# Order of the weight requests, PSUM banks and store queue around the early up-projection products of a hybrid encoder layer

## The chip, the core and the metric

The kernel runs on one core of one Trainium2 chip, as one launch. The metric is the device time of an execution in microseconds (us), the median of several runs. All engine times below are from one profiled execution of the kernel.

The engines are named as the profile names them: PE is TensorE (matmuls and transposes), PEld its weight load, DVE is VectorE, ACT is ScalarE, POOL is GpSimd, SP is SyncE, which here only issues DMAs. A name with a q (SPq, ACTq, POOLq) is the engine's queue issuing a DMA.

## What is computed

One encoder layer on 1024 tokens of width 1024, in float32. A token mixer (a gated delta rule beside a latent attention, both out of one input projection) ends in an output projection; after it comes a dense squared-ReLU MLP. The part that matters here:

```python
mixed = jnp.concatenate([o_gdn, o_mla], axis=-1) @ w_out
x = x + rms_norm(mixed, mix_post_norm)
h = rms_norm(x, ffn_pre_norm)
f = jnp.square(jax.nn.relu(h @ w_up)) @ w_down      # w_up: 1024 x 4096
x = x + rms_norm(f, ffn_post_norm)
```

## The kernel before, in words

Each float32 matmul is done as three passes on split operands (`mm3`, lines 206 to 209): an operand is kept as a high part (hi, cast on ACT) and a low part (lo, the rest, subtracted on DVE), and hi x hi, hi x lo and lo x hi are added up in PSUM. So every weight block is loaded into a raw tile, then split (`split_of`, lines 1323 to 1327: line 1325 on ACT, line 1326 on DVE).

**Out-projection and norms** (`out_proj`, line 1232). The 1024 tokens are eight blocks t of 128. For each block the projection adds two halves of 512 columns, each in one PSUM bank with the tag "out" (blocks 0 and 1 have theirs done earlier). `out_add` (line 1170) then adds a half to `part[t]` on DVE (line 1172) and squares it on ACT back into the bank (line 1173), which ends the use of the bank. The post norm, the residual and the pre norm follow on DVE (lines 1243 to 1251); line 1251 leaves the input of the MLP in `part[t]` and ends the use of the tile `xt`.

**Transposes** (`ffn_in`, line 1280, and `put`, line 1264). The up-projection is done with a Strassen-Winograd scheme of seven products on halves of the tokens and of the model width. Its moving operands are B11 and B21 (from blocks 0 to 3), and T1, T2, T3, T4 and B22 (from differences of blocks 4 to 7 with blocks 0 to 3, DVE lines 1291 to 1304; line 1294 writes a tile t2). `put` transposes 128 x 512 with four PE transposes (line 1268) into one of two "tr" banks and splits it (line 1273 on ACT, line 1274 on DVE). For t from 4 to 7 `ffn_in` is a generator that yields after each of its five puts.

**Pairs and early products.** The 4096 columns of w_up are 16 pairs p of 256 columns, each with two rows of weight tiles (512 KB each), `w_up[2p]` and `w_up[2p+1]`. Two of the seven products need only B11 and B21. For the eight even pairs they are computed ahead, by `filler` (line 1346): it requests `w_up[2p]`, splits it, runs twelve matmuls on B11 into a "ps" bank, copies the bank back into the first half of the raw tile (line 1355) and stores that half in DRAM (line 1356), runs twelve more on B21 onto the same bank, applies ReLU and square into the second half of the raw tile (lines 1363 and 1364) and stores it too (line 1365). The raw tile is free when both stores have landed. `fillers` (line 1368) chains the eight generators, each with four yields, and requests and splits the next one's row before it starts one. A regular pair is `up_pair` (line 1412); it needs `load_up(p)` (line 1387, both rows) and `prepare(p)` (line 1390), which forms on DVE a tile of sums (lines 1398 and 1399) and two differences (lines 1402 and 1405) and splits them. An even pair fetches its early products from DRAM (lines 1417 and 1418) and runs the remaining five products of twelve matmuls.

**What sets the order.** The order of each engine's queue is made when the kernel is built, from the order of the text as priority and from what is ready, so that products of later generators can stand ahead of earlier ones. All weight requests go through `load_chained` (line 182), which keeps those on SP's queue in the order of the text. Three buffer groups matter:
- "raw" (line 956): three tiles of 512 KB;
- "g" (line 1221): six tiles of 512 KB, for the two gain rows `gb` and `gf`, the eight `xt`, the t2 of blocks 4 to 7, four tiles of T3 that stay to the end of the up-projection, `sums`, and every fourth raw tile: `raw_of` (line 1317) takes a "g" tile where its running number leaves 3 when divided by 4;
- the weight pairs of `pair_tiles` (line 1312), five in turn: three of "whi"/"wlo", then "first", then "wv".

PSUM has eight banks. `psum_pool("psC", ...)` (line 1213) shares them out for this stretch: two "out", two "tr", four "ps".

**The order around the change** (lines 1462 to 1483). Blocks 0 to 7 go through `out_proj`, with the puts of blocks 0 to 3 between them and four steps of the early products at blocks 6 and 7. Then come `load_up(0)` and `prepare(0)`; then the five puts of each of blocks 4 to 7 with one step of the early products behind each put, and behind block 5 two steps of `prepare(0)`; then the remaining steps of the early products, the rest of `prepare(0)`, and the regular pairs. By the running number of `raw_of` the requests are: 1 and 2 for the first two early products, 3 ("g") and 4 for pair 0, 5 and 6 for the next two early products, 7 ("g") to 10 for the other four, 11 ("g") and 12 for pair 1.

Of the kernel before, what the change touches and what calls it, by code (L numbers as in the profile page):

```python
# [104 lines left out]
def build(tc, a, out):  # L105
    nc = tc.nc
# [15 lines left out]
    def psum_pool(name, **bufs):  # L122
        ps_stack.close()
        pp[:] = [ps_stack.enter_context(tc.tile_pool(name=name, bufs=1, space=PSUM, reuse_waits="tile")), bufs]
        for tag in bufs:
            psum2("order") if tag == "ps2" else psum("order", tag)
# [3 lines left out]
    def psum(name, tag="ps"):  # L130
        return pp[0].tile([P, HALF], F32, name=name, tag=tag, bufs=pp[1][tag])

    def psum2(name):
        return pp[0].tile([P, 2, HALF], F32, name=name, tag="ps2", bufs=pp[1]["ps2"])
# [71 lines left out]
    def mm3(ps, lhs, rhs, start, stop, **kw):  # L206
        mm(ps, lhs[0], rhs[0], start=start, stop=False, **kw)  # L207
        mm(ps, lhs[0], rhs[1], start=False, stop=False, **kw)  # L208
        mm(ps, lhs[1], rhs[0], start=False, stop=stop, **kw)  # L209
# [5 lines left out]
    def scratch(name, *shape):  # L215
        return dp.tile(list(shape), F32, name=name)
# [17 lines left out]
    d_p1 = [scratch(f"d_p1{p}", P, HALF) for p in range(NFILL)]  # L234
# [741 lines left out]
    def filler():  # L976
        yield "v1"
        yield from keys_values()

    def latent_side():  # L980
# [11 lines left out]
        + [substitute()]  # L992
        + [levels(h) for h in range(GH)]
        + [scan_loads(), scan(), filler(), latent_side(), projections()]
    )
    LB.close()
# [213 lines left out]
            out_pairs(early[t][:, n], t, n, (NPAIR - 1,))  # L1210
            out_add(early[t][:, n], t, n, ss1[t])
    L.close()
    psum_pool("psC", out=2, tr=2, ps=4)


    L = ExitStack()
# [3 lines left out]
    def gtile(name, dt=F32):  # L1220
        return gp.tile([P, D], dt, name=name, tag="g", bufs=6)
# [38 lines left out]
    def moving(block, k):  # L1260
        n = 4 // len(block)
        return cut(block[k // n], slice(None), k % n)
# [13 lines left out]
    first_half, second_half = slice(0, HALF), slice(HALF, D)  # L1276
# [3 lines left out]
    def ffn_in(t):  # L1280

        h = part[t]
        if t < 4:
            put(B11, h[:, first_half], t)
            put(B21, h[:, second_half], t)
            return
        if t == 4:
            later.update(T1=big("T1", bp, "b"), B22=big("B22", bp, "b"), T2=halves_of("T2", mtile))
        o, c = part[t - 4], t - 4
        t2 = gtile("t2")[:, :HALF]  # L1290
        nc.vector.tensor_sub(o[:, first_half], h[:, first_half], o[:, first_half])
        put(later["T1"], o[:, first_half], c)
        yield
        nc.vector.tensor_sub(t2, h[:, second_half], o[:, first_half])
        put(later["T2"], t2, c)
        yield
        nc.vector.tensor_sub(o[:, second_half], o[:, second_half], t2)
        if t == 4:
            later.update(T4=halves_of("T4", mtile), T3=halves_of("T3", gtile))
        put(later["T4"], o[:, second_half], c)  # L1300
        yield
        put(later["B22"], h[:, second_half], c)
        yield
        nc.vector.tensor_sub(h[:, first_half], h[:, second_half], h[:, first_half])
        put(later["T3"], h[:, first_half], c)
        part[t] = part[t - 4] = None
        yield
# [9 lines left out]
    def raw_of(src):  # L1317
        raws[0] += 1
        r = gtile("raw") if raws[0] % 4 == 3 else raw_tile()
        load_chained(r, src)  # L1320
        return r

    def split_of(raw, n=D, eng=None):
        hi, lo = pair_tiles()
        nc.scalar.copy(hi[:, :n], raw)  # L1325
        (eng or nc.vector).tensor_tensor(lo[:, :n], raw, hi[:, :n].bitcast(F32), op=ALU.subtract)
        return hi, lo

    def k_slice(w, half, k):
        return cut(w, slice(None), slice(half * HALF + k * P, half * HALF + (k + 1) * P))  # L1330
# [12 lines left out]
    def early_pair(p):  # L1343
        return p % 2 == 0

    def filler(p):
        x = raw_of(a["w_up"][2 * p])
        w = split_of(x)
        yield
        ps = psum("ps_up")  # L1350
        for k in range(4):
            mm3(ps, k_slice(w, 0, k), moving(B11, k), k == 0, k == 3)
            if k == 1:
                yield
        nc.scalar.copy(x[:, first_half], ps)
        nc.gpsimd.dma_start(d_p1[p // 2], x[:, first_half])
        yield
        for k in range(4):
            mm3(ps, k_slice(w, 1, k), moving(B21, k), False, k == 3, skip_group_check=True)
            if k == 1:  # L1360
                yield
        square_of = x[:, second_half]
        nc.scalar.activation(square_of, ps, AF.Relu)
        nc.scalar.activation(square_of, square_of, AF.Square)
        nc.gpsimd.dma_start(act_block(p, 0), square_of)
        yield

    def fillers():
        gens = [filler(p) for p in range(NPR) if early_pair(p)]
        run(gens[0])  # L1370
        for n, g in enumerate(gens):
            run(gens[n + 1] if n + 1 < len(gens) else None)
            for _ in g:
                yield

    def act_block(p, j):
        return d_act[p // 2][j, :, (p % 2) * HALF : (p % 2 + 1) * HALF]
# [9 lines left out]
    def load_up(p):  # L1387
        loaded[p] = raw_of(a["w_up"][2 * p]), raw_of(a["w_up"][2 * p + 1])

    def prepare(p):  # L1390

        r1, r2 = loaded.pop(p)
        w = wts[p] = {}
        if not early_pair(p):
            w["A1"] = split_of(r1)
        yield
        s = gtile("sums")
        nc.vector.tensor_add(s[:, first_half], r2[:, first_half], r2[:, second_half])
        nc.vector.tensor_sub(s[:, second_half], s[:, first_half], r1[:, first_half])
        w["S12"] = split_of(s)  # L1400
        yield
        nc.vector.tensor_sub(r2[:, first_half], r1[:, first_half], r2[:, first_half])
        w["S3A"] = split_of(r2)
        yield
        nc.vector.tensor_sub(r1[:, second_half], r1[:, second_half], s[:, second_half])
        w["S4"] = split_of(r1[:, second_half], HALF)

    def run(g):
        if g is not None:
            next(g, None)  # L1410
# [51 lines left out]
    fill = fillers()  # L1462
    for t in range(NT):
# [4 lines left out]
        if t >= 6:  # L1468
            run(fill)
            run(fill)  # L1470
    load_up(0)
    ahead = prepare(0)
    for t in range(4, NT):
        for _ in ffn_in(t):
            run(fill)
        if t == 5:
            run(ahead)
            run(ahead)
    for _ in fill:
        pass  # L1480
    for _ in ahead:
        pass
    psum_pool("psD", ps=8)
# [54 lines left out]
    for p in range(NPR):  # L1538
        if p + 1 < NPR:
            ahead = prepare(p + 1)  # L1540
        else:
            ahead = None
# [160 lines left out]
```

## Time and profile before

| | us |
|---|---|
| median of three runs (1301.52 to 1306.1) | 1303.38 |
| profiled execution | 1300.08 |
| its span | 1298.4 |
| PE busy | 1229.7 (95% of the span) |
| DVE busy | 905.7 (70%) |
| ACT busy | 652.3 (50%) |
| POOL busy | 172.7 (13%) |
| mean granted PE clock | 0.979 of full speed |

In the stretch from 540 to 760 us the DMA view lists 20 requests of w_up rows by SP (512 KB each), eight stores of line 1356 by POOL (256 KB, 2.6 us from issue to landing in the median) and eight of line 1365 by POOL (256 KB, 2.9 us).

In a row of the timeline stand the start in us, the duration in us, the engine, the line, the operation, the tile written and the tiles read (buffer numbers left out), the shapes, and the count; in square brackets the idle time of the engine before it and what ended it. Lines 207, 208 and 209 are the three passes of `mm3`, so products are told apart by their tiles: a "ps_up" matmul that reads B11 or B21 belongs to an early product as long as the early products run, and one that reads T1 opens a regular even pair. In the chain of waits each row is a piece of the chain that ended last: its start, its length, and the work that it is. Matmuls overlap, so a matmul's step is read from the starts.

### The profile page before, as it was taken

Reading aid. Unit: us, or ns where it says so; the run is one execution under the profiler, and the core shown is the slowest. Engines: PE = TensorE matmul, PEld = TensorE weight load, DVE = VectorE, ACT = ScalarE, POOL = GpSimd, SP = SyncE. Lnnn points to the kernel's source line nnn. Section 1 sums busy time; section 2 is a strip of 40 time slices with the busy share of each in tenths; the row PEclk is TensorE's granted clock in tenths of the full one; section 3 lists DMA queues with packets and bytes.
Section 4 is the critical chain, followed back from the end, with each engine's and each line's share of the span. In section 5 each row is a group of like instructions: output and inputs, shape, how many; then the busy total and the mean of one; then the engine's idle time right before and its main releaser. Section 6 shows DMA issues by size and latency. Waiting matters only on the chain.

```text
span 1298.4 us, 17709 instructions
## 1 busy us (share of the span) xinstructions
PE 1229.7 (95%) x6224; PEld 1038.4 (80%) x6224; DVE 905.7 (70%) x1779; ACT 652.3 (50%) x1189; POOL 172.7 (13%) x168
## 2 busy tenths in 40 slices
PE   7999999999899899998777999999999999999995
PEld 6978888899778788877665888888887888888884
DVE  7678879546655876778955677677765686775844
ACT  6566743426655776754544354454445433344431
POOL 1011011220055443420001000000000000011021
PEclk9999999999999999999988999999999999999998
DMA  5114545645243511305523355555539984556802
GB/s 229 53 63 138 183 130 204 191 114 163 88 121 119 144 30 29 93 14 194 203 105 104 124 186 186 187 186 187 187 138 374 383 314 140 191 170 218 329 28 97
DMA packets 110193, 205.71 MB, mean 158 GB/s; under 512 B 33557, under 2 KB 51989, under 8 KB 110106
## 3 DMA queue, kind: packets, MB, share of 16 engines
q1 hardware_dynamic: 94848, 176.09, 40.4%
q10 hardware_dynamic: 13978, 24.31, 5.1%
q0 software_dynamic: 1280, 4.20, 0.8%
q8 instruction: 49, 0.80, 0.2%
q14 instruction: 38, 0.31, 0.1%
HBM read 143.07 MB, written 61.49 MB: 158 GB/s over the span
## 4 chain that ended last, share of the span: by engine, by line
PE 61%; DVE 4%; DMA 3%; issue 2%; ACT 2%; POOL 0%; SPq 0%; DVEq 0%; ACTq 0%; POOLq 0%
PE ps_dn L209 8%; PE ps_dn L208 8%; PE ps_up L207 7%; PE ps_dn L207 7%; PE ps_up L209 7%; PE ps_up L208 7%; PE ps_out L207 2%; PE ps_out L209 2%; PE ps_out L208 2%; PE ps_PT L1061 2%; PE ps_o L1080 1%; PE ps_sc L207 1%; DMA raw<-in_w_up_dram 1%; PE ps_o L1079 1%; PE ps_sc L208 1%
## 5 line engine op out<-in xcount | busy, mean ns | idle before, releaser
L1574 POOL TENSOR_TENSOR rows<-rows,gpost 128x512 f32<-128x512 f32 x16 | 23.9, 1512 | 553.3 <-ACT junk L1571 553.3
L209 PE MATMUL ps_proj<-hThi,wlo 128*128 128x512 f32 x192 | 75.1, 395 | 1.2 <-DVE wlo L199 1.2
L208 PE MATMUL ps_proj<-hTlo,whi 128*128 128x512 f32 x192 | 76.0, 396 | 0.0
L207 PE MATMUL ps_proj<-hThi,whi 128*128 128x512 f32 x192 | 76.0, 396 | 0.0
L1065 DVE TENSOR_TENSOR PTlo<-ps_PT,PThi 128x512 fp32r<-128x512 f32 (+2 forms) x96 | 52.0, 550 | 20.0 <-ACT PThi L1064 19.3
L1064 ACT CAST PThi<-ps_PT 128x512 fp32r<-128x512 f32 (+2 forms) x96 | 45.4, 481 | 29.9 <-PE ps_PT L1061 28.4
L1506 DVE TENSOR_TENSOR dlo<-draw,dhi 128x1024 fp32r<-128x1024 f32 x35 | 44.7, 1302 | 22.3 <-ACT dhi L1505 22.3
L208 PE MATMUL ps_dn<-dlo,dhi 128*128 128x512 f32 x144 | 56.0, 389 | 0.0
L209 PE MATMUL ps_dn<-dhi,dlo 128*128 128x512 f32 x144 | 56.0, 389 | 0.0
L207 PE MATMUL ps_dn<-dhi 128*128 128x512 f32 x144 | 55.5, 389 | 0.0
L1035 ACT ACTIVATE Pt<-ps_sc,nm 128x896 f32<-128x896 f32 (+3 forms) x64 | 48.0, 750 | 11.8 <-DVE nm L1033 7.6
L1325 ACT CAST whi<-raw 128x1024 fp32r<-128x1024 f32 (+1 forms) x28 | 24.9, 898 | 55.5 <-PE ps_up L208 54.0
L1505 ACT CAST dhi<-draw 128x1024 fp32r<-128x1024 f32 x35 | 36.1, 1048 | 33.1 <-issue 13.8
L1061 PE MATMUL ps_PT<-ident,Pt 128*128 128x128 f32 x288 | 46.4, 275 | 3.1 <-DVE PTlo L1065 1.8
L1033 DVE TENSOR_REDUCE nm<-ps_sc 128x1 f32<-128x896 f32 (+3 forms) x64 | 47.8, 750 | 1.2
L1040 POOL TENSOR_TENSOR Pt<-Pt,rs 128x128 f32<-128x128 f32 (+4 forms) x40 | 35.4, 884 | 88.5 <-DVE rs L1038 64.4
L199 DVE TENSOR_TENSOR wlo<-raw,whi 128x1024 fp32r<-128x1024 f32 (+1 forms) x27 | 33.9, 1259 | 17.8 <-ACT whi L198 15.2
L209 PEld LDWEIGHTS ps_proj<-hThi,wlo 128*128 128x128 f32 x192 | 36.1, 188 | 9.1 <-DVE wlo L199 1.7
L1079 PE MATMUL ps_o<-PThi,V 128*128 128x256 f32 (+1 forms) x160 | 40.5, 276 | 3.0 <-DVE o L1086 1.2
L208 PEld LDWEIGHTS ps_proj<-hTlo,whi 128*128 128x128 f32 x192 | 36.1, 188 | 7.4 <-issue 0.5
L207 PEld LDWEIGHTS ps_proj<-hThi,whi 128*128 128x128 f32 x192 | 36.1, 188 | 7.4 <-issue 0.5
L1061 PEld LDWEIGHTS ps_PT<-ident,Pt 128*128 128x128 f32 x288 | 34.0, 140 | 8.4 <-issue 2.4
(591 smaller groups left out, 3999.2 us busy)
## 6 DMA issues: line engine op xcount, KB each, us to landing
draw<-in_w_down_dram SPq DMA_DIRECT2D x47, 512.0 KB
draw<-d_act SPq DMA_DIRECT2D x41, 512.0 KB
raw<-in_w_up_dram SPq DMA_DIRECT2D x40, 512.0 KB
raw<-in_w_down_dram SPq DMA_DIRECT2D x17, 512.0 KB
raw<-in_w_qkvg_dram SPq DMA_DIRECT2D x16, 512.0 KB
d_act<-c SPq DMA_DIRECT2D x16, 512.0 KB
d_act<-s SPq DMA_DIRECT2D x16, 512.0 KB
raw<-d_act SPq DMA_DIRECT2D x15, 512.0 KB
```

The source lines that it names most:

```text
L207: mm(ps, lhs[0], rhs[0], start=start, stop=False, **kw)
L208: mm(ps, lhs[0], rhs[1], start=False, stop=False, **kw)
L209: mm(ps, lhs[1], rhs[0], start=False, stop=stop, **kw)
L1033: nc.vector.tensor_reduce(nm, ps[:, :npc, :w], axis=AX.XY, op=ALU.max, negate=True)
L1035: nc.scalar.activation(Pt[:, :n].rearrange("p (i w) -> p i w", i=npc), ps[:, :npc, :w], AF.Exp, bias=nm, scale=1.0, accum_out=sm)
L1040: nc.gpsimd.tensor_tensor(Pt[:, :n], Pt[:, :n], rs.to_broadcast([P, n]), op=ALU.mult)
L1061: transpose(ps[:, j * P : (j + 1) * P], Pt[:, b * P : (b + 1) * P], ident)
L1064: nc.scalar.copy(hi[:, :n, cs], ps3)
L1065: nc.vector.tensor_sub(lo[:, :n, cs], ps3, hi[:, :n, cs].bitcast(F32))
L1079: mm(ps[:, cs], V[h][:, b], hi[:, cs], start=(b == 0), stop=False)
L1505: nc.scalar.copy(hi, raw)
L1506: nc.vector.tensor_tensor(lo, raw, hi.bitcast(F32), op=ALU.subtract)
```

## The change

Three things are changed.
- The psC pool gives four banks to "out" and two to "ps"; "tr" keeps two.
- The two stores of each early product are issued by ACT instead of POOL.
- `load_up(0)` and `prepare(0)` move from ahead of the puts of block 4 to behind those of block 7 and one more step of the early products. Two steps of `prepare(0)` then go behind the next two steps of the early products, and the rest behind the last.

By the running number of `raw_of` the requests become: 1 and 2 for the first two early products, 3 ("g") to 6 for the next four, 7 ("g") and 8 for the last two, 9 and 10 for pair 0, 11 ("g") and 12 for pair 1.

```diff
@@ -1210,7 +1210,7 @@
     L.close()
-    psum_pool("psC", out=2, tr=2, ps=4)
+    psum_pool("psC", out=4, tr=2, ps=2)
@@ -1353,7 +1353,7 @@
         nc.scalar.copy(x[:, first_half], ps)
-        nc.gpsimd.dma_start(d_p1[p // 2], x[:, first_half])
+        nc.scalar.dma_start(d_p1[p // 2], x[:, first_half])
         yield
@@ -1362,7 +1362,7 @@
         nc.scalar.activation(square_of, ps, AF.Relu)
         nc.scalar.activation(square_of, square_of, AF.Square)
-        nc.gpsimd.dma_start(act_block(p, 0), square_of)
+        nc.scalar.dma_start(act_block(p, 0), square_of)
         yield
@@ -1468,16 +1468,15 @@
-    load_up(0)
-    ahead = prepare(0)
     for t in range(4, NT):
         for _ in ffn_in(t):
             run(fill)
-        if t == 5:
+    run(fill)
+    load_up(0)
+    ahead = prepare(0)
+    for n, _ in enumerate(fill):
+        if n < 2:
             run(ahead)
-            run(ahead)
-    for _ in fill:
-        pass
     for _ in ahead:
         pass
     psum_pool("psD", ps=8)
```

## Prediction

> **What bounds the kernel now.** The page shows TensorE (PE) busy in nearly every slice of the span, so time can be won only where PE waits. I therefore divided the stretch around the change into windows of 20 us. The columns are the window, then busy us and instructions of PE, PEld, DVE, ACT and POOL, then the granted PE clock, the DMA share and GB/s.
>
> ```profile
> 620.00:640.00 20.00, 19.35 (x90) 15.46 (x88) 19.71 (x48) 11.96 (x28) 1.81 (x3) 1.00 0.51 176
> 640.00:660.00 20.00, 13.71 (x52) 10.28 (x52) 16.22 (x33) 8.40 (x18) 1.62 (x3) 0.74 0.44 156
> 660.00:680.00 20.00, 15.13 (x63) 11.01 (x61) 7.52 (x13) 9.33 (x18) 1.64 (x4) 0.83 0.36 129
> 680.00:700.00 20.00, 14.01 (x54) 11.42 (x55) 11.05 (x16) 7.60 (x12) 1.60 (x3) 0.74 0.17 66
> 700.00:720.00 20.00, 15.28 (x71) 12.42 (x70) 9.78 (x17) 9.68 (x20) 2.17 (x4) 0.83 0.48 158
> 720.00:740.00 20.00, 20.00 (x90) 16.58 (x89) 15.21 (x22) 8.07 (x11) 0.00 (x0) 1.00 0.34 124
> ```
>
> From 640 to 720 PE idles about 22 us and runs at 0.74 to 0.83 of its clock; from 720 on, with the regular pairs, it is full. There it waits for no transfer (DMA share 0.34), so what is gained before 720 should reach the end. Next, PE's timeline in that stretch, to see each wait and its releaser (start, duration, instruction, idle before it).
>
> ```profile
> 639.48 0.60 PE L1268 MATMUL ps_h2T<-ident,part 128*128 128x128 f32 x4
> ...
> 648.05 0.79 PE L207 MATMUL ps_up<-B11hi,first_hi 128*128 128x512 f32 x1 [2.55 <-ACT first_hi L1325]
> ...
> 666.33 1.16 PE L1268 MATMUL ps_h2T<-ident,part 128*128 128x128 f32 x8 [1.75 <-DVE T2lo L1274]
> 668.76 0.79 PE L207 MATMUL ps_up<-B11hi,whi 128*128 128x512 f32 x1 [1.26 <-ACT whi L1325]
> ...
> 673.60 0.63 PE L208 MATMUL ps_up<-B11lo,whi 128*128 128x512 f32 x1
> 674.02 0.63 PE L209 MATMUL ps_up<-B11hi,wlo 128*128 128x512 f32 x1
> ...
> 685.99 0.79 PE L207 MATMUL ps_up<-B11hi,whi 128*128 128x512 f32 x1 [7.60 <-ACT whi L1325]
> ...
> 691.28 0.61 PE L208 MATMUL ps_up<-B11lo,first_hi 128*128 128x512 f32 x1
> ...
> 713.80 1.11 PE L1268 MATMUL ps_h2T<-ident,part 128*128 128x128 f32 x4 [3.99 <-DVE B22lo L1274]
> 714.56 0.78 PE L207 MATMUL ps_up<-T1hi,whi 128*128 128x512 f32 x1
> ...
> 718.55 0.63 PE L207 MATMUL ps_up<-T1hi,whi 128*128 128x512 f32 x1
> ```
>
> I call the eight early products E0 to E7 (pairs 0, 2, ... 14). E0 and E1 end at 639.48, E2 starts at 648.05, E4 at 668.76, E5 at 685.99, and the first regular pair (pair 0) at 714.56. Behind a wait the matmuls are slow for a while: twelve from 668.76 to 674.02, thirteen from 685.99 to 691.28, ten from 714.56 to 718.55, one every 0.42 us (673.60 and 674.02). At full clock, in E0:
>
> ```profile
> 634.04 0.39 PE L207 MATMUL ps_up<-B21hi,whi 128*128 128x512 f32 x1
> 634.26 0.39 PE L208 MATMUL ps_up<-B21lo,whi 128*128 128x512 f32 x1
> ```
>
> That is 0.22 us a matmul, so each slow one costs 0.20 us on top of the wait ahead of it. An early product, 24 matmuls, is 5.4 us at full clock (0.225 each). Of the 75.1 us from 639.48 to 714.56, six products take 32.4 and twenty groups of four transposes, some 0.5 each (eight take 1.16 at 666.33, at a low clock), 10: about 42.4 us are work, and 32.7 are idle time and slow clock.
>
> Third, the chain of waits, for what is behind the releasers.
>
> ```profile
> 639.40 2.47 DMA d_act<-raw
> 642.00 4.93 DMA raw<-in_w_up_dram
> 646.96 1.05 ACT first_hi L1325
> ...
> 664.18 3.46 DMA raw<-in_w_up_dram
> ...
> 679.98 2.30 DMA d_act<-raw
> 682.50 0.70 DVE sums L1398
> 683.22 0.70 DVE sums L1399
> 683.95 2.00 ACT whi L1325 x2
> ```
>
> These are buffer waits. E2's rows could be requested only when E0's store had landed (642.00), because pair 0's two rows had taken one "g" slot and the third "raw" slot:
>
> ```profile
> 633.77 0.83 SPq L183 DMA_DIRECT2D raw<-in_w_up_dram  x2
> ```
>
> E4 takes a "g" slot at 664.18. Pair 0's sums need a "g" slot too and wait 4.4 us for E4's store (682.50); E5's cast is queued on ACT behind the cast of these sums (683.95 x2), hence 7.60 us. The DVE rows show that "g" slots go out in the order of the text:
>
> ```profile
> 639.33 1.28 DVE L1251 SCALAR_TENSOR_TENSOR part<-xt,rffn,gffn 128x1024 f32<-128x1024 f32 x1
> ...
> 659.10 0.42 DVE L1274 TENSOR_TENSOR T3lo<-ps_h2T,T3hi 128x256 fp32r<-128x256 f32 x1 [0.44 <-ACT T3hi L1273]
> 659.44 0.68 DVE L1294 TENSOR_TENSOR t<-part,part 128x512 f32<-128x512 f32 x1
> ...
> 687.30 0.69 DVE L1294 TENSOR_TENSOR t<-part,part 128x512 f32<-128x512 f32 x1
> ...
> 710.91 0.69 DVE L1398 TENSOR_TENSOR sums<-raw 128x512 f32<-128x512 f32 x1 [2.72 <-DMA raw<-in_w_up_dram]
> ```
>
> The t2 of token block 5 comes directly behind the last of block 4's T3 tiles (659.44), that of block 6 only when the sums are split (687.30). The first row ends the use of an xt slot at 640.61.
>
> **The change part by part.** *The order of requests.* The early products advance in quarter steps. By the code, E6's row is requested at the 21st step of the early products, E7's at the 25th, and pair 0's rows follow. All requests form one chain on SP, so this order holds whatever else moves. E2 now takes the "g" slot that pair 0 held, E3 the free "raw" slot, E4 and E5 those of E0 and E1.
>
> E2: the slot comes behind block 4's t2. Of the four xt slots one came free at 633.77 and the next at 640.61, so the request goes out by 640.6 instead of 642.00, and with E3's it has no store to wait for; with 3.46 to 4.93 us of load and 1.05 of cast E2 starts between 638.5 and 648. I take 646, nearest to the later request: 2.0 us gained.
>
> E4 and E5 are requested at 642 and land with E2 and E3 by about 650 (four loads, none over 4.93 alone), under 10.9 us of E2 and E3. So the 1.75 and 1.26 us near 668 go, with twelve slow matmuls (2.4): 5.4. E5 waits for no sums: 7.60 and thirteen slow matmuls (2.6): 10.2. With t2 of blocks 6 and 7 no longer behind the sums, their transposes come some 20 us sooner, and so the 3.99 us at 713.80, where DVE had stood 2.72 us before a regular pair's row with B22's subtraction behind it, go too, with ten slow matmuls (2.0): 6.0. Sum of the gains: 23.6 us.
>
> What is late next: E6 takes a "g" slot behind t2 of block 7, at about 666 (three blocks after 659.44), landed by 671; E2 to E5 with the transposes of the blocks keep PE until 677. That covers it with 5 us to spare. Pair 0's second row takes E5's slot. From E5's last matmul on: relu, square, store, load, sums, cast. The rows of E4 have the first three.
>
> ```profile
> 678.43 0.60 ACT L1363 ACTIVATE raw<-ps_up 128x512 f32<-128x512 f32 x1 [1.68 <-PE ps_up L209]
> ```
>
> From the relu's start at 678.43 to the sums at 682.50 are 4.1 us; with 3.46 to 4.93 of load, 1.4 of sums and 1.05 of cast this is 10.0 to 11.5 us, against E6 and E7 with 10.9. E7 can't start before E5's bank is free, so its 5.4 us of this cover are certain and E6's nearly; without E6's, 6 us are lost. I take 2 us lost (0 to 6). The sums, subtractions and splits are the same ones as before, now beside E7 instead of ahead of E5; of them only the first split is needed at the start of pair 0. Pair 1's rows wait for E7's slot: 4.1 us of store and 4.93 of load, 9 us into pair 0, whose five products of twelve matmuls last 13.5: hidden. On SP pair 0's two requests are moved past six others (E2 to E7), and nothing else is queued behind them before pair 0 runs.
>
> *The stores on ACT.* Sixteen issues move from POOL, which has little else to do there (under 2.2 us in each window), to ACT. An issue of ACT's, and the shortest, median and longest of one kind of SP's (ns):
>
> ```profile
> 606.27 0.33 ACTq L1247 DMA_DIRECT2D d_x<-xt  x1
> ```
>
> ```profile
> L183 SPq DMA_DIRECT2D raw<-d_q x8: 444/451/1213, 243.1 to 500.5; - x8
> ```
>
> ACT gains 5.3 us of work in windows where it is busy under half. Behind each issue stand casts of transposes and weights, for which DVE and PE wait: 0 to 16 x 1.21 = 19.4 us; a store that lands sooner could give a few tenths back. I take 1 us, near the 0.33 row, with most of it hidden. The Trainium skill, DMA: Bandwidth & Descriptors, Issuing engines are not separate DMA queues, speaks against this part: all issuers share the same 16 DMA engines, so a move saves only issue time, and here it is taken from an idle POOL. By it the move is worth no more than nothing, which the 1 us lost agrees with.
>
> *The banks.* Out-projection waits for a bank once, visibly:
>
> ```profile
> 594.74 0.50 PE L207 MATMUL ps_out<-whi,first_hi 128*128 128x512 f32 x1 [3.65 <-ACT ps_out L1173]
> ...
> 626.49 1.03 PE L1268 MATMUL ps_h2T<-ident,part 128*128 128x128 f32 x8
> ```
>
> ```profile
> 622.28 1.28 DVE L1251 SCALAR_TENSOR_TENSOR part<-xt,rffn,gffn 128x1024 f32<-128x1024 f32 x1
> ```
>
> With four banks PE is ahead by 3.65 us and some slow clock. But E0 needs block 3's transposes (626.49), whose norm DVE ends at 623.56 (622.28). So at most 2.9 us arrive, and none if DVE, which is busy 19.71 of 20 us from 620 to 640, sets the pace: I take 1. Early products keep a bank until the relu (0.60); while one is emptied, the half of another (2.7 us) runs, so two banks suffice: 0, or 6 x 0.60 = 3.6 lost.
>
> **Sum:** 23.6 + 1 - 2 - 1 = 21.6 us. The profiled execution took 1300.08 (its span is 1298.4), which becomes 1278.5; it lies 3.3 below the median of 1303.38, so 1281.8. The other end of the gains is all 32.7 us and 2.9 of the banks: about 1268.
>
> The Trainium skill, TensorE: Matmul & The Clock Gate, Part 1, has the clock fall to one half after an idle window of about 3.4 us. The trace agrees on the half (0.22 against 0.42) but shows twelve slow matmuls behind 1.26 us of idle time at 668.76. By the page only the waits of 7.60 and 3.99 would carry slow clock, and the time would be 1284 (12 x 0.20 = 2.4 us less gained), an estimate by that page.
>
> **The rivals.** *Part of the gain is taken back at E6* (chance 0.14). If t2 of blocks 6 and 7 is slow, E6's request comes at 680, not 666; it starts at 686, nine us after E5's end, with twelve slow matmuls: 11.4 less, a gain of 10, 1293. For it: the slots go out in text order. Against it: nothing but the sums stood ahead of block 6.
>
> *No change: two banks* (0.10). If the products are not interleaved, each of the six waits for relu and semaphore (about 1 us) and starts with twelve slow matmuls (2.4): 20 us, the whole gain, 1302. For it: 1.26 us of idle time was enough to slow the clock. Against it: E2 and E3 were interleaved by halves. The same page of the Trainium skill, A second HAM failure mode: psum-queue depth-cycling, describes short waits on banks that keep the clock oscillating; no wait on these banks is in this trace, so none bears it out yet.
>
> *Slower: ACT's queue* (0.13). If the issues on ACT last 1.21 us each and stand ahead of casts that PE waits for, 19.4 us are lost, and four of the waits bring slow clock (4 x 2.4 = 9.6): 29 against 21.6, 1311. It turns slower from about 0.75 us an issue on with all on the path. Against it: 0.33 in the ACT rows, and transposes that can be reordered round it.
>
> **How the numbers follow.** The main case, gains of 13 to 34 us, has 0.63; with the first rival faster is 0.77. Within 0.3% (3.9 us, about what a measurement of this kernel can tell from no change) is 0.10, slower 0.13. The range of 1269 to 1304 leaves out the slower rival, part of the no-change case and the last of the gains.
>
> **What would show it.** Right: pair 0's first ps5 matmul near 693 or before, no PE wait above 3 us from 650 on, requests of E2 to E5 in one group by 643, and the wait of sums on d_act gone. Wrong: E6's cast waiting for its row behind a late t2, PE waiting for relu at the starts of E2 to E7, or ACT's issues well over 0.33 us with casts late behind them.

## The result and the profile after

The changed kernel takes 1280.94 us (median of four runs, 1278.62 to 1281.83) against 1303.03 us for the kernel before (four runs, 1301.52 to 1306.1): 22.1 us less, a ratio of 0.9828 with a 95% interval of 0.9807 to 0.9849. The profiled execution took 1280.36 us, its span is 1278.6 us and its mean granted PE clock 0.985.

The same windows as before the change, for the changed kernel:

```profile
620.00:640.00 20.00, 13.90 (x59) 11.36 (x58) 20.00 (x48) 11.03 (x25) 0.00 (x0) 0.83 0.52 187
640.00:660.00 20.00, 20.00 (x95) 16.59 (x94) 17.87 (x34) 12.66 (x24) 0.00 (x0) 1.00 0.53 185
660.00:680.00 20.00, 14.97 (x82) 12.16 (x80) 10.49 (x21) 9.80 (x22) 0.00 (x0) 0.93 0.38 135
680.00:700.00 20.00, 19.14 (x85) 15.19 (x86) 13.03 (x19) 11.86 (x22) 0.00 (x0) 0.90 0.46 165
700.00:720.00 20.00, 20.00 (x89) 16.44 (x89) 18.62 (x28) 9.61 (x13) 0.00 (x0) 1.00 0.45 162
```

PE is now busy for 88.0 of these 100 us, where it had been for 77.5. Two holes are left, one in the first window and one in the third. PE's timeline shows what they are:

```profile
630.03 1.94 PE L1268 MATMUL ps_h2T<-ident,part 128*128 128x128 f32 x8 [6.10 <-DVE rpost_v L172]
631.79 1.22 PE L207 MATMUL ps_up<-B11hi,whi 128*128 128x512 f32 x2
...
645.26 0.39 PE L207 MATMUL ps_up<-B11hi,first_hi 128*128 128x512 f32 x1
...
648.43 0.60 PE L1268 MATMUL ps_h2T<-ident,part 128*128 128x128 f32 x4
...
670.24 0.60 PE L1268 MATMUL ps_h2T<-ident,part 128*128 128x128 f32 x4
672.29 1.09 PE L1268 MATMUL ps_h2T<-ident,part 128*128 128x128 f32 x8 [1.45 <-DVE B22lo L1274]
674.79 0.66 PE L1268 MATMUL ps_h2T<-ident,t 128*128 128x128 f32 x4 [1.40 <-DVE T1lo L1274]
675.28 0.60 PE L1268 MATMUL ps_h2T<-ident,part 128*128 128x128 f32 x4
677.32 1.94 PE L1268 MATMUL ps_h2T<-ident,part 128*128 128x128 f32 x8 [1.44 <-DVE T2lo L1274]
680.34 0.80 PE L207 MATMUL ps_up<-B11hi,whi 128*128 128x512 f32 x1 [1.08 <-ACT whi L1325]
...
696.09 0.48 PE L207 MATMUL ps_up<-T1hi,wv_hi 128*128 128x512 f32 x1
```

E2 starts at 645.26 without a wait, and E2 to E5 run to 670.24 without one; the waits of 2.55, 1.26 and 7.60 us are gone. Pair 0 opens at 696.09, where it had opened at 714.56. The hole that is new stands ahead of E6 (680.34): from 670.24 on PE has only seven of the twenty groups of transposes (670.24 to 677.32; some 3 us at 0.44 us each) in 10.1 us. The chain of waits says what that stretch hangs on:

```profile
671.55 0.70 DVE B22lo L1274
672.29 1.11 PE ps_h2T L1268 x8
673.42 0.59 ACT T1hi L1273
674.04 0.70 DVE T1lo L1274
674.79 0.67 PE ps_h2T L1268 x4
675.51 3.70 DMA raw<-in_w_up_dram
679.24 1.05 ACT whi L1325
680.34 0.80 PE ps_up L207
```

Read upwards: E6 waits for its cast, the cast for its row, and the row was requested only at 675.51, when PE had read the third of the four t2 tiles (the transposes of `t` at 674.79, the only ones in this stretch). By the profile it is these transposes that SP's request waited for, so that tile held the "g" slot; the fourth t2 had got its slot sooner (667.24 below). The transposes, in turn, wait for DVE's splits to free one of the two "tr" banks. SP's requests show two groups: the four rows of E2 to E5 (two at 634.03 and 634.41, the other two at 647.0 and 649.0), and ten rows from E6's on.

```profile
634.03 15.26 SPq L183 DMA_DIRECT2D raw<-in_w_up_dram  x4
675.51 31.37 SPq L183 DMA_DIRECT2D raw<-in_w_up_dram  x10
```

DVE's rows: block 3's norm, the t2 of block 4, the other three t2, and the first sums, which no longer wait for a store.

```profile
628.60 1.28 DVE L1251 SCALAR_TENSOR_TENSOR part<-xt,rffn,gffn 128x1024 f32<-128x1024 f32 x1
...
642.02 0.69 DVE L1294 TENSOR_TENSOR t<-part,part 128x512 f32<-128x512 f32 x1
...
663.00 1.28 DVE L1294 TENSOR_TENSOR t<-part,part 128x512 f32<-128x512 f32 x2
...
667.24 0.69 DVE L1294 TENSOR_TENSOR t<-part,part 128x512 f32<-128x512 f32 x1 [1.75 <-PE ps_h2T L1268]
...
688.85 0.69 DVE L1398 TENSOR_TENSOR sums<-raw 128x512 f32<-128x512 f32 x1 [1.29 <-PE ps_h2T L1268]
```

And one of the store issues on ACT, all of which last 0.33 to 0.36 us:

```profile
644.92 0.33 ACTq L1365 DMA_DIRECT2D d_act<-raw  x1
```

For the experiments a mark is needed that leaves out the time before the change. One out-projection matmul has the same place in every kernel; here it is in the profile of before and then in that of the changed kernel:

```profile
582.72 0.49 PE L207 MATMUL ps_out<-whi,mixhi 128*128 128x512 f32 x1 [0.70 <-ACT ps_out L1173]
```

```profile
584.59 0.49 PE L207 MATMUL ps_out<-whi,mixhi 128*128 128x512 f32 x1 [0.70 <-ACT ps_out L1173]
```

From it to the opening of pair 0 are 131.84 us before (714.56) and 111.50 after (696.09). I call this the stretch.

### The profile page after: what moved, and what is told of

Read it like the earlier page. It is cut to its first block, busy times and chain, and to the rows that moved or that the text cites. A ratio compares the mean times of both kernels' runs of the same rounds, so it can differ in the third digit from the quotient of the medians.

```text
span 1278.6 us, 17685 instructions
## 1 busy us (share of the span) xinstructions
PE 1222.9 (96%) x6224; PEld 1035.5 (81%) x6224; DVE 903.9 (71%) x1779; ACT 651.9 (51%) x1189; POOL 163.4 (13%) x152
## 4 chain that ended last, share of the span: by engine, by line
PE 60%; DVE 5%; DMA 3%; ACT 2%; issue 1%; POOL 1%; SPq 0%; DVEq 0%; ACTq 0%; POOLq 0%
PE ps_up L207 8%; PE ps_up L209 8%; PE ps_up L208 8%; PE ps_dn L208 8%; PE ps_dn L209 8%; PE ps_dn L207 8%; PE ps_PT L1061 2%; PE ps_out L207 2%; PE ps_out L208 1%; PE ps_out L209 1%; PE ps_o L1080 1%; PE ps_sc L207 1%; PE ps_o L1079 1%; PE ps_sc L208 1%; PE ps_sc L209 1%
## 5 line engine op out<-in xcount | busy, mean ns | idle before, releaser
L209 PE MATMUL ps_proj<-hThi,wlo 128*128 128x512 f32 x192 | 75.1, 395 | 1.2 <-DVE wlo L199 1.2
L1080 PE MATMUL ps_o<-PTlo,V 128*128 128x256 f32 (+1 forms) x160 | 41.2, 300 | 0.0
```

The lines of the kernel that those rows point to most:

```text
L1080: mm(ps[:, cs], V[h][:, b], lo[:, cs], start=False, stop=(b == nb - 1))
```

## The experiments

All fourteen kernels, with the median of four runs each (ten for e2 and e3), the ratio to the runs of the kernel before that were made beside them, and the stretch in the profiled run. The medians of the kernel before beside the experiments lie between 1301.78 and 1303.03 us, so times from different rows compare to about 1 us.

| kernel | order | banks out/tr/ps | stores on | other | us | ratio, 95% interval | stretch |
|---|---|---|---|---|---|---|---|
| before | old | 2/2/4 | POOL | | 1303.03 | | 131.84 |
| changed | new | 4/2/2 | ACT | | 1280.94 | 0.9828, 0.9807 to 0.9849 | 111.50 |
| e1 | new | 2/2/4 | POOL | | 1284.70 | 0.9859, 0.9831 to 0.9888 | 115.44 |
| e2 | old | 4/2/2 | POOL | | 1300.50 | 0.9985, 0.9969 to 1.0001 | 131.94 |
| e3 | old | 2/2/4 | ACT | | 1298.72 | 0.9980, 0.9959 to 1.0002 | 129.62 |
| e4 | new | 2/2/4 | ACT | | 1280.06 | 0.9843, 0.9807 to 0.9878 | 112.86 |
| e5 | new | 4/2/2 | POOL | | 1281.21 | 0.9841, 0.9824 to 0.9859 | 113.18 |
| f1 | loads old, sums new | 2/2/4 | POOL | | 1289.10 | 0.9899, 0.9883 to 0.9916 | 121.37 |
| f2 | new | 4/2/2 | ACT | t2 in "m" | 1287.93 | 0.9889, 0.9872 to 0.9906 | 117.82 |
| e8 | new | 4/2/2 | ACT | E6 in "raw" | 1284.75 | 0.9868, 0.9852 to 0.9885 | 115.44 |
| g1 | new | 2/4/2 | ACT | | 1276.97 | 0.9800, 0.9780 to 0.9819 | 106.32 |
| g2 | new | 2/4/2 | ACT | t2 in "m" | 1270.96 | 0.9756, 0.9732 to 0.9780 | 100.41 |
| h1 | new | 2/4/2 | POOL | t2 in "m" | 1270.61 | 0.9773, 0.9743 to 0.9802 | 99.68 |
| h2 | old | 2/4/2 | ACT | t2 in "m" | 1286.81 | 0.9887, 0.9871 to 0.9904 | 120.66 |

My theory was that the order of the requests and sums makes the gain; the rivals were that the banks or the stores make it. Four kernels take the change apart.

**e1, the order alone.** The changed kernel with the other two parts undone:

```diff
-    psum_pool("psC", out=4, tr=2, ps=2)
+    psum_pool("psC", out=2, tr=2, ps=4)
-        nc.scalar.dma_start(d_p1[p // 2], x[:, first_half])
+        nc.gpsimd.dma_start(d_p1[p // 2], x[:, first_half])
-        nc.scalar.dma_start(act_block(p, 0), square_of)
+        nc.gpsimd.dma_start(act_block(p, 0), square_of)
```

> Only the requests and the preparation of pair 0 move; banks 2/2/4 and stores on POOL as before. My theory (the whole gain is in the order of the requests): 1277 to 1285 us, 18 to 26 below the kernel before, and pair 0 opens near 692 to 697. Rival (out-projection's banks are what PE gained on): within 4 us of 1303. Rival (stores that land sooner free the raw tiles): above 1290.

**e2, the banks alone**, in the kernel before:

```diff
-    psum_pool("psC", out=2, tr=2, ps=4)
+    psum_pool("psC", out=4, tr=2, ps=2)
```

> Only the banks change, to 4/2/2. My theory: the wait of 3.65 us ahead of 594.74 goes, but DVE sets when block 3 is ready, so E0 starts no earlier and the time is 1301 to 1307. Rival (banks): 1283 to 1295. Rival (two banks hold the early products up): 1308 or more, with PE waiting for the relu at the start of E2 to E7.

**e3, the stores alone**, in the kernel before:

```diff
-        nc.gpsimd.dma_start(d_p1[p // 2], x[:, first_half])
+        nc.scalar.dma_start(d_p1[p // 2], x[:, first_half])
-        nc.gpsimd.dma_start(act_block(p, 0), square_of)
+        nc.scalar.dma_start(act_block(p, 0), square_of)
```

> Only the sixteen stores move from POOL to ACT. My theory: 1300 to 1305; each raw tile comes free some tenths sooner, and ACT pays 0.33 us an issue beside its other work. Rival (sooner landing is the gain): 1285 to 1297. Rival (ACT's queue holds the casts up): 1308 or more, with issues of 0.6 us and longer.

**e4, the changed kernel without its banks:**

```diff
-    psum_pool("psC", out=4, tr=2, ps=2)
+    psum_pool("psC", out=2, tr=2, ps=4)
```

> The changed kernel with the banks back at 2/2/4. The changed kernel's profile shows PE waiting 6.1 us for block 3's norm with four banks, and E0 starting 4 us later than before. If that loss reaches the end: 1275 to 1278. If E6's wait for its row takes it up again, since that row waits for a t2 tile and not for PE: 1279 to 1283. Rival (the banks brought gain): 1286 or more.

Measured: the order alone takes 18.0 of the 22.1 us (1302.67, the median of before beside it, to 1284.70). Its pair 0 opens at 701.79, not at 692 to 697; the mark lies 3.6 us later in that run than before, which explains part of it. The banks alone and the stores alone leave the time within what can be told from no change; both intervals reach 1. e4 lands between 1279 and 1283, the case in which E6's late row takes up what the banks lose. In e2 the waits ahead of E2, E5 and pair 0 are still there, and a new one stands at the start. PE's timeline of e2:

```profile
631.73 1.94 PE L1268 MATMUL ps_h2T<-ident,part 128*128 128x128 f32 x8 [6.09 <-DVE rpost_v L172]
...
653.37 0.79 PE L207 MATMUL ps_up<-B11hi,first_hi 128*128 128x512 f32 x1 [2.17 <-ACT first_hi L1325]
...
687.14 0.80 PE L207 MATMUL ps_up<-B11hi,whi 128*128 128x512 f32 x1 [9.48 <-ACT whi L1325]
...
714.47 1.11 PE L1268 MATMUL ps_h2T<-ident,part 128*128 128x128 f32 x4 [4.55 <-DVE B22lo L1274]
```

So four banks let PE end the out-projection sooner, and then it waits 6.09 us for block 3's norm, which DVE reaches late. The next question was what in the order makes the gain: the slots that pair 0's rows held, or the work of the sums ahead of E5.

**f1, the rows early, the sums late**, in the kernel before:

```diff
     load_up(0)
     ahead = prepare(0)
     for t in range(4, NT):
         for _ in ffn_in(t):
             run(fill)
-        if t == 5:
-            run(ahead)
-            run(ahead)
-    for _ in fill:
-        pass
+    run(fill)
+    for n, _ in enumerate(fill):
+        if n < 2:
+            run(ahead)
```

> The kernel before with one edit: the two steps of prepare(0) that stood behind block 5 go behind the last early products, as in the change, while load_up(0) stays where it was, so pair 0's two rows hold one "g" and one "raw" slot all the while. Theory of the slots: E2 still waits for E0's store and E4 for its slot, only E5's wait for the cast of the sums (7.60 us and thirteen slow matmuls) and the late t2 go: some 10 to 12 us less than before, 1291 to 1293, and the matmul with which pair 0 opens 121 us behind the first early out-projection matmul (131.8 in the kernel before, 115.4 in the run of the order alone). Rival, that the work of the sums ahead of E5 in ACT's and DVE's queues is all of it: as the order alone, 1285, 115 us.

PE's timeline of f1:

```profile
649.86 0.79 PE L207 MATMUL ps_up<-B11hi,first_hi 128*128 128x512 f32 x1 [2.91 <-ACT first_hi L1325]
...
670.46 0.80 PE L207 MATMUL ps_up<-B11hi,whi 128*128 128x512 f32 x1 [1.34 <-ACT whi L1325]
```

E2's and E4's waits are close to those of before (2.55 and 1.26), as the theory of the slots has it, and no wait of 7.60 us follows. The stretch is 121.37 as that theory said: 10.5 us of it go with the sums, and e1's 115.44 gives the slots 5.9. These 5.9 are net of a new loss: in e1, as in the changed kernel, E6's row stands behind a t2, in f1 it doesn't. Both parts act, the sums more. The time, 1289.10, is 2 to 4 us below the 1291 to 1293 expected, 13.1 less than before.

Then the hole ahead of E6. Two kernels take its row out from behind the last t2.

**f2, t2 in another group of tiles**, and **e8, another early product in "g"**, both edits to the changed kernel:

```diff
-        t2 = gtile("t2")[:, :HALF]
+        t2 = mtile("t2", F32)[:, :HALF]
```

> The changed kernel with one edit: the t2 tiles come from the 16 tiles of the group "m" instead of "g", so that E6's row takes a "g" slot that the gain rows leave when block 7 is normed. Theory that E6's wait is the slot behind t2 of block 7: E6's row is requested by about 660 instead of 675.5, E6's matmuls fill the waits among the last transposes (670 to 680 us, of which some 3 us are work), and the time falls by 5 us (3 to 7), to 1276; pair 0 opens 106 us behind the first early out-projection matmul instead of 111.5. Rival, that the transposes' round trips over two banks between PE, ACT and DVE set that stretch: E6's row comes early and pair 0 opens as late as before, 1281.

```diff
-        r = gtile("raw") if raws[0] % 4 == 3 else raw_tile()
+        r = gtile("raw") if raws[0] % 4 == 0 else raw_tile()
```

> The changed kernel with one edit: the raw tile that comes from the group "g" is the fourth of four instead of the third, so E3's and E7's rows take "g" slots and E6's takes the "raw" slot of E2, free about 659. Theory that E6's wait is the slot behind t2 of block 7: E6 is requested by 660, only E7 waits for that slot (675), covered by E6's 5.4 us in part: 3 us less than the changed kernel, 1278, and no wait of over 1.5 us at E6's start. Rival, the round trips of the transposes: 1281, no difference.

Both theories missed: f2 is 7.0 us slower than the changed kernel and e8 3.8 us slower. In e8 the "g" slot was only handed to another row: E3's is requested at 652.47, the requests of E4 and E5 go out behind it on SP's chain, and PE waits 3.43 us at 655.88, by the profile for the second of the four t2. What held E3's request so long isn't shown. In f2 the hole is gone, with PE full from 640 to 680, but a larger one opens later. PE's timeline of f2, then DVE's:

```profile
686.00 1.06 PE L1268 MATMUL ps_h2T<-ident,part 128*128 128x128 f32 x4 [3.73 <-DVE T1lo L1274]
690.45 1.09 PE L1268 MATMUL ps_h2T<-ident,part 128*128 128x128 f32 x4 [3.38 <-DVE T2lo L1274]
...
700.80 0.78 PE L207 MATMUL ps_up<-T1hi,wv_hi 128*128 128x512 f32 x1
```

```profile
679.30 0.69 DVE L1398 TENSOR_TENSOR sums<-raw 128x512 f32<-128x512 f32 x1 [2.11 <-issue]
...
683.51 1.83 DVE L1326 TENSOR_TENSOR wlo<-raw,whi 128x1024 fp32r<-128x1024 f32 x2 [0.24 <-ACT whi L1325]
685.26 0.68 DVE L1274 TENSOR_TENSOR T1lo<-ps_h2T,T1hi 128x512 fp32r<-128x512 f32 x1
```

With E6 and E7 run early, pair 0's rows come early too; DVE does their sums and splits (679.30 to 685.3) ahead of T1's split, and the transposes behind it wait for the bank. By then no early product is left beside them. The late row of E6 had kept two products back as work to lie beside the last transposes. This reading is argued from the rows. From it came another theory: what is dear is the last transposes' way through two banks, and the early products are only what covers it.

**g1 and g2, four banks for the transposes**, in the changed kernel and in f2:

```diff
-    psum_pool("psC", out=4, tr=2, ps=2)
+    psum_pool("psC", out=2, tr=4, ps=2)
```

> The changed kernel with other banks: two for out-projection, four for the transposes, two for the early products. If the waits of PE among the last transposes (672 to 680 us: 1.45, 1.40, 1.44 us and the slow clock beside them) come from the two "tr" banks, each of which is free only when ACT and DVE have split it, they shrink with four banks, t2 of block 7 and with it E6's request come some 3 us sooner, and the time is 1278 (1276 to 1280); if the order of the work on ACT and DVE sets them, no difference, 1281.

> The kernel with t2 in "m" (1287.9 us: E6 and E7 run early there and the transposes of blocks 5 to 7 stand alone from 682 to 701, with waits of PE of 3.73, 3.38, 0.78, 1.16 us and a clock of 0.65) with two banks for out-projection, four for the transposes and two for the early products. Theory that those transposes cost so much because nothing is left beside them and only two banks keep them going: with four banks they take about half as long, 6 to 8 us less, 1281. Rival, that the rows of pair 0 or the sums are what comes last there: 1288, no difference.

g1 came out as expected, though its interval overlaps that of the changed kernel; g2 gains 17 us on f2, more than twice what was expected. The two edits make a square: t2 in "m" alone costs 7.0 us, these banks alone bring 4.0, both together bring 10.0. The edit also takes two banks from the out-projection, and with them goes the wait of 6.10 us ahead of E0: E2 starts 61.9 us behind the mark in f2 and 59.8 in g2, so some 2 of the 17 us may be due to that. Against e4, which leaves the out-projection the same two banks, g1's row of E6 is requested 88.7 us behind the mark instead of 91.2, and the stretch is 6.5 us shorter. The rest of g2's gain comes later, where with four banks the transposes are done among the early products: in g2 the last t2 is transposed at 679.69, ahead of pair 0's first sums at 683.11, with PE not waiting. Then E6's early row is worth having. The windows of g2:

```profile
640.00:660.00 20.00, 20.00 (x101) 16.36 (x100) 18.65 (x35) 13.28 (x26) 0.00 (x0) 1.00 0.59 208
660.00:680.00 20.00, 20.00 (x110) 16.68 (x109) 17.17 (x35) 13.65 (x32) 0.00 (x0) 1.00 0.61 209
```

g2 beats both kernels, by 32 us the one before and by 10 the changed one.

**e5 and h1, the stores back on POOL**, in the changed kernel and in g2; **h2, g2 in the old order** (`load_up(0)`, `prepare(0)` and its steps where they were before). The edit of e5 and h1:

```diff
-        nc.scalar.dma_start(d_p1[p // 2], x[:, first_half])
+        nc.gpsimd.dma_start(d_p1[p // 2], x[:, first_half])
-        nc.scalar.dma_start(act_block(p, 0), square_of)
+        nc.gpsimd.dma_start(act_block(p, 0), square_of)
```

> The changed kernel with one edit: the two stores of each early product are issued by POOL again, as before. If the stores on ACT give what they gave beside the old banks (run without the banks against run of the order alone: 4.6 us in the medians, 2.9 on the pair-0 mark), this takes 1284 to 1285 and pair 0 opens 114 us behind the first early out-projection matmul; the row of E6 is requested some 3 us later than in the changed kernel. If it was the variation between compilations of the order alone, 1281 and 111.5.

> The fastest kernel so far (t2 in "m", two banks for out-projection, four for the transposes, two for the early products: 1270.96 us) with the sixteen stores of the early products issued by POOL again. In the pairs of runs so far the stores on ACT were worth 4.6 us beside the old banks and nothing beside the change's. If a store from ACT frees its raw tile sooner and that is what counts, a loss of 2 to 4 us, 1273 to 1275. If the earlier difference came from another order of transposes and matmuls that the compilation happened to give, either sign and under 2 us: 1269 to 1273.

The edit of h2:

```diff
+    load_up(0)
+    ahead = prepare(0)
     for t in range(4, NT):
         for _ in ffn_in(t):
             run(fill)
-    run(fill)
-    load_up(0)
-    ahead = prepare(0)
-    for n, _ in enumerate(fill):
-        if n < 2:
+        if t == 5:
             run(ahead)
+            run(ahead)
+    for _ in fill:
+        pass
```

> The same fastest kernel with load_up(0) and prepare(0) back where they were before the change. Theory that the place of pair 0's rows and sums costs what the pieces showed in the kernel before (the sums ahead of E5 some 10.5 us, the two slots some 6): 1271 + 16 = 1287. Rival, that with t2 out of "g" and four banks for the transposes those waits are covered by other work, so that the move is hardly needed: 1275 or less.

Neither e5 nor h1 differs from its pair by what can be told (0.3 us above and 0.4 below); of the two larger differences the intervals overlap (e1 to e4, 4.6 us) or reach no change (e3, 0.2%). So no effect of the queue is shown. What e1 to e4 may be worth goes with a later E6: in e1 E6's row is requested 93.9 us behind the mark, in e4, e5 and the changed kernel 90.9 to 91.2. Why it is later there stays open.

h2 lands on the theory's number: 1286.81 for 1287. The wait ahead of E5 is back, and so is, smaller than the 4.37 us of before, that of the sums for a store. PE's timeline of h2, then DVE's:

```profile
683.32 0.79 PE L207 MATMUL ps_up<-B11hi,whi 128*128 128x512 f32 x1 [9.20 <-ACT whi L1325]
```

```profile
679.83 0.69 DVE L1398 TENSOR_TENSOR sums<-raw 128x512 f32<-128x512 f32 x1 [0.77 <-DMA d_act<-raw]
```

The move is worth 15.9 us even where the banks and slots are better.

## Why the prediction was right, and where its steps were not

The forecast of 1281.8 us is 0.9 above the measured 1280.94, but so close a hit is luck: it is a sum of errors that cancel. The order alone was put at 21.6 (23.6 less 2) and brought 18.0; banks and stores were put at nothing together, and the changed kernel stands 3.8 us below e1. Each of the two stands 3.5 (e5) to 4.6 (e4) below e1 and both together no more; all these intervals overlap, so the 3.8 us can't be shared out, nor told from nothing.

**Two terms of about 8 us cancel.** The first is E2's. Its gain was put at 2.0 us, but before the change more was lost around E2 than its own wait of 2.55, as PE had nothing else to do beside the transposes:

```profile
642.55 0.63 PE L1268 MATMUL ps_h2T<-ident,t 128*128 128x128 f32 x4 [2.47 <-DVE t L1294]
644.42 1.09 PE L1268 MATMUL ps_h2T<-ident,part 128*128 128x128 f32 x4 [1.23 <-DVE rffn_v L172]
...
653.74 0.83 PE L1268 MATMUL ps_h2T<-ident,part 128*128 128x128 f32 x4
```

From E1's end (639.48) to the end of E2's first half (653.74) are 14.3 us, with three groups of transposes and twelve slow matmuls, which at the prediction's own prices are 4.2 us of work: some 10 us were lost. In the changed kernel one group and the same twelve matmuls take 3.2 us (645.26 to 648.43): nothing is lost. With the order alone (e1) E2 starts 58.6 us behind the mark instead of 65.3. The second term is the hole ahead of E6, put at nothing: 7 us, and seven slow matmuls behind it at 0.20 us, 1.4. So from E1's end to the opening of pair 0 the changed kernel takes 24.3 us less (75.1 before, 50.8 after), where the prediction had 23.6 less 2.

**The main cause holds.** Pair 0's slots and sums made the waits; the order alone brings 18.0 us and 16.4 of the stretch. By parts: the sums and the late t2 were put at 10.2 + 6.0 = 16.2 us and measured 10.5 (f1); the slots were put at 2.0 + 5.4 = 7.4 and measured 5.9 (f1 to e1), net of the hole ahead of E6.

**E2's request.** It was put at 640.6, behind block 4's t2, because slots "go out in the order of the text". It came at 634.03, and t2 was written only at 642.02: the slot that came free went to the row, not to t2. This step was wrong, though E2's start was forecast at 646 and came at 645.26, right behind E1 and without a wait. E4's and E5's requests, put at 642, went out at 647.0 and 649.0, so the sign "in one group by 643" was not met; PE waited for none of these rows.

**E6, the step that failed by size.** "E6 takes a g slot behind t2 of block 7, at about 666 ... That covers it with 5 us to spare", and no loss; the 2 us lost were for pair 0's rows. The time of t2's subtraction was about right: the last three begin at 663.00 and 667.24. But the slot that E6's row took, that of the third t2, was free only when PE had transposed the tile, at 674.79, since the last transposes wait in turn for two banks. And E2 to E5 ended at 670.24, not 677, as only seven of the twenty groups of transposes had been run among them. The hole is 10.1 - 3 = 7 us, and the clock is 0.93 and 0.90 in the two windows there. The first rival described this: it had the request at 680 and E6 nine us after E5's end; it was 675.51 and 10.1 us, of which transposes fill 3. Its condition, a late t2, didn't hold: what came late was the t2's last reader. And the slot alone is not the cure, as f2 showed. The prediction had priced the transposes by their work on PE (0.5 us a group) and never asked what a group waits for when nothing runs beside it.

**Pair 0's rows.** Hidden as forecast: pair 0 opens at 696.09, behind the last early product and transposes; it was forecast near 693, and the mark lies 1.9 us later than before.

**The banks.** One us was taken, within 0 and 2.9. In the medians the changed kernel stands 0.9 us above e4: nothing that can be told. The way was named in the prediction as the bound ("none if DVE ... sets the pace"): DVE is busy 20.00 of 20 us from 620 to 640 and reaches block 3's norm at 628.60, having been at 622.28. E0 starts 47.2 us behind the mark instead of 45.0 (631.79 and 627.76), behind a wait of 6.10 us, and ten slow matmuls follow. At the end it isn't seen: the stretch is 111.50, and 112.86 without these banks; that E6's late row takes it up is argued, not shown. That the early products can do with two banks was right here: PE shows no wait for a relu in the changed kernel. In g1, which also leaves them two, one wait of 1.61 us for a relu shows at 660.10.

**The stores.** One us lost was taken; no pair of kernels shows a loss. The issues last 0.33 to 0.36 us on ACT as in the row used (one in e4 0.91), and the rival of 1.21 us is out. The Trainium skill, DMA: Bandwidth & Descriptors, Issuing engines are not separate DMA queues, holds the move to be worth no more than issue time. The two pairs at 0.3 and 0.4 us agree; the pairs with old banks, at 2.6 to 4.6 us better, would speak against it but can't be told from no change with their intervals.

**The clock.** The prediction let short waits cost slow matmuls, the shortest of 1.26 us ahead of E4. Read in finer windows, the granted clock before is 0.50 from 667.9 to 674.7, so it fell when that wait had barely begun; in the 3.4 us ahead of the fall PE was busy for 1.24. In the changed kernel the clock is 0.50 from 677.0 to 683.8, behind 3.4 us in which PE was busy for 1.09, among waits of 1.40 and 1.44; E6's first seven matmuls (680.34 to 683.47) are slow, at 0.43 us a step or more. g1, with waits of 0.94, 0.96 and 0.76 in the same stretch, keeps a clock of 1.00. So what went ahead of the slow clock here is not one wait of a certain length but a few us with little work. The Trainium skill, TensorE: Matmul & The Clock Gate, Part 1, has the clock fall after an idle window of about 3.4 us; in the two cases above PE was busy for about a third of such a time, so the trace does not agree that it must be idle throughout.

## What to carry to other kernels

A tile is in use until its last reader has run, so when the next user of a slot can start is read from that reader's row, not from the row that fills the tile. Before a wait is taken away, ask what the work it held back was covering: here a row that came sooner cost 7 us until the transposes had banks enough to run among the matmuls, and then it brought 6. Work on small tiles that goes through several engines is priced by its round trip and its buffers, not by its time on the busiest engine.

## What was not expected of the hardware

The mark itself lies between 582.29 and 586.99 us in the fourteen profiled runs, though none of the edits touches the work ahead of it: single spans differ by some 4.7 us from what happened earlier, which is as much as some of the parts are worth. The stretch between two marks is the better measure for those, though each stretch here is from a single execution. And it varies too: behind the same wait of 3.65 us early in the out-projection the clock is 0.50 for 3.4 us before the change (596.2 to 599.6) and for 6.8 us in f1 (594.1 to 600.9), and E0 starts 45.0 us behind the mark in the one and 46.1 in the other.
